# VectorE transposes squares of 32x32 for the norms' scales, the parameters and part of x

## The chip, the core and the metric

The kernel runs on one core of a Trainium2 chip. The core has a matrix engine (TensorE, "PE" in the profile; its weight loads are "PEld"), a vector engine (VectorE, "DVE"), an activation engine (ScalarE, "ACT"), GpSimd ("POOL") and a sync engine ("SP") that here only issues DMAs. Each engine runs its own instructions in the order in which the program wrote them; they wait for each other through semaphores. The metric is the time of one execution in microseconds on the device.

## What is computed

One layer of a decoder on 256 positions of 1024 columns, in float32: a norm, attention with 16 heads of 64, a projection and a residual, a second norm, a gated feed-forward net with a causal convolution of width 3, a residual and a last norm. With 256 positions there is one block of keys only, so the block-sparse attention is ordinary causal attention with a bias by distance.

```python
def rms_norm(x, g):
    y = xf * lax.rsqrt(jnp.mean(xf * xf, axis=-1, keepdims=True) + NORM_EPS)
    return (y * g.astype(jnp.float32)).astype(x.dtype)

y = rms_norm(h, attn_norm[i])
qkv = (y @ w_qkv[i]).reshape(B, S, 3, N_HEADS, HEAD_DIM)
o = moba_attention(q, k, v, rel_bias)      # softmax(q k / 8 + bias, causal) v
h = h + o.transpose(0, 2, 1, 3).reshape(B, S, D) @ w_o[i]
y = rms_norm(h, ffn_norm[i])
# conv_ffn: u = y @ w_up; u = conv over 3 positions + conv_b; (silu(gate) * val) @ w_down
h = h + conv_ffn(y, w_up[i], conv_w[i], conv_b[i], w_down[i])
return rms_norm(h, final_norm)
```

## The kernel before

**Layout.** x lies in `xs` as two row tiles of 128 positions by 1024 columns. A product needs its input with the contracted dimension on partitions, so the normed x is kept transposed in `yt`: 8 blocks of 128 columns, each 128 x 256 positions. The norm's per-column weight (`g1`, `g2`) is multiplied in when a block is transposed; its per-position scale (1 / root of the mean square) is not. It is multiplied in after the products: for V, whose positions lie on partitions, as a scalar per partition; for queries, keys and the feed-forward net, whose positions lie along the free dimension, it must stand in every partition as a row of 256 numbers (`rk`, `rq`, `rb2`).

**Split products.** TensorE multiplies in a shortened float format. Each operand is therefore split into a part in that format and the rest (`yt[:, 0]` and `yt[:, 1]`; `whi` and `wlo` for weights), and each product is three matmuls: first with first, rest with first, first with rest. ACT casts a weight tile to `whi` (line 144) and DVE subtracts to give `wlo` (line 157). One cast and one subtraction make a unit; `unit(n)` puts n of them where they are called, in the order of the table `groups`: V's weights, queries and keys by head pair, the output projection, then up and down. A raw weight tile is one of four; when its second unit is written, the next load is issued on SP's queue (`load_next`), and it starts when the tile's readers are done. SP's first loads are, in order: x's columns 0 to 255, weight rows for V, x's columns 256 to 511, weight rows for V, x's columns 512 to 1023 (line 187), the next weight rows for V (line 98), and so on.

**Order.** Nothing is scheduled by a planner: `manual_schedule` keeps the order of the code on every engine.
- V first: `transposed(k)` turns two blocks of x on TensorE into PSUM (line 260); ACT writes `yt[:, 0]` (264), DVE `yt[:, 1]` (267). Steps i = 0 to 3 of the loop at line 376 transpose the next two blocks, multiply the two blocks at hand with V's weights into four accumulators `acc`, and put units behind that.
- After the last step but one, ACT has the squares, DVE adds (`rstds`, 239), POOL raises to the power -0.5 (240), and DVE scales the identity with the result (`diagonals`, 252). `spread` multiplies ones with these on TensorE, which gives the scale in every partition; DVE copies it from PSUM to `rk` (404) and makes `rq` (405). V is read out of `acc` by ACT (401) and DVE (403).
- Heads follow in three steps of 2, 3 and 3 pairs: `project` gives a pair's queries and keys, which DVE multiplies with `rq` (439) and `rk` (442); `scores`, softmax, a turn of the weights (partly by a 32x32 transpose on DVE over all 128 partitions, line 484, and DMAs), and `mix` one step later, written out by ACT (525) and DVE (526).
- Parameters of the feed-forward net (convolution weights, its bias, `ffn_norm`) are loaded as rows and transposed by `other_params` on TensorE (225), in step i = 2 of V's loop; ACT copies them to `params` (226) and scales `g2` (227).
- The second norm: TensorE transposes blocks 4 to 7, and multiplies the first two tiles of `up` (`first[0]`, `first[1]`, two PSUM banks). Between their halves stands the second `spread`; DVE copies it to `rb2` (700). For each tile j, DVE reads the bank as `u` = bank x `rb2` (656), and the convolution and gate follow. There are two banks, so tile j + 2 waits for the `u` of tile j.
- The end: `finish` is called for each row tile. It takes POOL's power (739), scales the row (DVE 512 columns at line 743, ACT twice 256 at line 746) and issues three DMAs (747, 748).

Of the kernel before, what the change touches and what calls it, by code (L numbers as in the profile page):

```python
# [8 lines left out]
F32 = mybir.dt.float32  # L9
# [5 lines left out]
P = 128  # L15
S = 256
# [31 lines left out]
def tile_block(ctx: ExitStack, tc, x, attn_norm, w_qkv, w_o, rel_bias, ffn_norm, w_up, conv_w,  # L48
# [20 lines left out]
    def spare():  # L69
        return psT.tile([P, 512], F32, name="spare")  # L70

    def mm(o, lhsT, rhs, start, stop):
        nc.tensor.matmul(o, lhsT, rhs, start=start, stop=stop, skip_group_check=True)  # L73
# [148 lines left out]
    def other_params():  # L222
        ps = spare()[:, :2 * P].rearrange("p (a b) -> p a b", a=2)
        for i in range(2):
            nc.tensor.transpose(ps[:, i, :], rows[:, i, :], ident)  # L225
        nc.scalar.activation(params, ps, AF.Copy)
        nc.scalar.activation(g2, g2, AF.Copy, scale=math.sqrt(D))
# [5 lines left out]
    small.tile([P, 104], F32, name="gap", bufs=1)  # L233
# [9 lines left out]
    def spread(d, ps):  # L243

        for t in range(NT):
            mm(ps[:, t * P:(t + 1) * P], ones, d[t], True, True)
        return ps[:, :S]

    def diagonals(r):
        d = [small.tile([P, P], F32, name=f"diag{t}", bufs=1) for t in range(NT)]  # L250
        for t in range(NT):
            nc.vector.tensor_scalar(d[t], ident, r[:, t:t + 1], None, op0=ALU.mult)
        return d
# [15 lines left out]

    def transposed(k, g, ps=None):  # L270

        ps = flipped_rows(k, ps)
        for part in (columns_hi, columns_lo):
            for a in range(2):
                part(ps, k, g, a)
# [79 lines left out]

    ps = flipped_rows(0)
# [19 lines left out]
    for i in range(4):  # L376
        if i < 3:
            transposed(2 * i + 2, g1)
        if i == 2:
            other_params()  # L380
        for kk in range(2):
            k = 2 * i + kk
            if k:
                rows_product(accs, yt[:, :, k, :], ("v", i), kk, CHAINS, False, k == KD - 1)
        if i:
            unit(2)
        else:
            for _ in range(2):
                split_hi()
                split_lo()  # L390
        if i == 1:
            nc.scalar.activation(junk[0], xt[0], AF.Square, accum_out=stat[:, 0, 0:1])
        if i == 2:
            nc.scalar.activation(junk[1], xt[1], AF.Square, accum_out=stat[:, 0, 1:2])
            r1 = rstds()
            d1 = diagonals(r1)
    ps = spread(d1, bank())
# [6 lines left out]
    nc.vector.tensor_copy(rk, ps)  # L404
# [131 lines left out]
    for step in STEPS:  # L536
# [10 lines left out]
        for j, p in enumerate(step):  # L547
            split_to(("qk", p))
            for which in range(2):
                state["by"] = nc.gpsimd if last and 2 * j + which < 3 else nc.vector  # L550
                project(p, which)
                if not (step == STEPS[1] and (j, which) == (2, 1)):
                    unit(2 if not last and which == 0 else 1)
# [142 lines left out]
    up_k(1, first[1], range(0, 4))  # L696
    up_k(0, first[0], range(4, 8))
    ps = spread(diagonals(rstds()), acc())
    unit(2)
    nc.vector.tensor_copy(rb2, ps)  # L700
    up_k(1, first[1], range(4, 8))
# [32 lines left out]
    def finish(t, n):  # L734
# [8 lines left out]
        nc.vector.tensor_scalar(o[:, 512:], xg[t][:, 512:], r, None, op0=ALU.mult)  # L743
        for q, b in ((nc.sync, 0), (nc.scalar, 256)):
            c = slice(b, b + 256)
            nc.scalar.activation(o[:, c], xg[t][:, c], AF.Copy, scale=r)  # L746
            q.dma_start(rows[:, c], o[:, c])
        nc.sync.dma_start(rows[:, 512:], o[:, 512:])
# [66 lines left out]
```

## Time and profile before

| | before |
|---|---|
| time, median of 3 runs | 301.33 us (299.57 to 301.43) |
| the profiled execution's own time | 301.26 us |
| its span, from the first instruction to the last | 299.5 us |
| TensorE (PE) busy | 291.8 us, 97% |
| VectorE (DVE) busy | 229.9 us, 77% |
| ScalarE (ACT) busy | 170.7 us, 57% |
| mean granted TensorE clock | 0.996 of full |

All engines' times are microseconds from the span's start. A row of the trace gives the start, the length, the engine, the line, the operation, the tile written and the tiles read, the shape and the count. Brackets at its end hold the time for which the engine was idle before the row and what ended that. Neighbouring equal instructions are merged into one row with a count (x2), whose length goes from the first one's start to the last one's end. In the chain of waits a row holds the start, the length and the place of a piece of the work that ended last. A row of stretches gives each engine's busy time in a stretch, with the number of instructions, then the granted clock, the DMA engines' busy share and GB/s.

### The profile page before, as it was taken

The page shows a single profiled execution, that of the slowest core. Times are in us where ns is not written, and L with a number is a line of the kernel's source. Part 1 is how long each engine was busy: PE and PEld are TensorE (multiplying, and loading weights), DVE is VectorE, ACT ScalarE, POOL GpSimd, SP SyncE. Part 2 cuts the span into 40 slices and gives each one's busy share as a digit, 9 for nine tenths or more (in the row PEclk, how much of TensorE's full clock was granted, in tenths as well). Part 3 has the DMA queues.
Part 4 walks back from the last instruction along what each step waited for, and adds up shares of the span by engine and source line. Part 5 has one row for each costly group of instructions (what it writes and reads, how often), then busy time and mean ns, then how long its engine had stood idle before and what let it go on. Part 6 is the DMA issues. An engine that isn't in the chain of part 4 may idle for free.

```text
span 299.5 us, 5466 instructions
## 1 busy us (share of the span) xinstructions
PE 291.8 (97%) x2116; PEld 269.6 (90%) x2116; DVE 229.9 (77%) x428; ACT 170.7 (57%) x311; POOL 32.1 (11%) x61
## 2 busy tenths in 40 slices
PE   8999999999999999999999999999999999999992
PEld 7888989989978789998989899999989898999881
DVE  2666888569598585999895959988795959599751
ACT  4485837339265677477582727756474727275241
POOL 4703006418200001000000000000000000000010
PEclk9999999999999999999999999999999999999998
DMA  6999397798896964274939092976364748400011
GB/s 222 414 385 297 133 368 218 188 407 214 246 383 155 325 211 177 88 239 141 344 128 327 24 349 63 317 239 229 130 220 135 265 142 279 144 0 2 0 70 70
DMA packets 44245, 62.07 MB, mean 207 GB/s; under 512 B 1772, under 2 KB 37308, under 8 KB 44220
## 3 DMA queue, kind: packets, MB, share of 16 engines
q1 hardware_dynamic: 42492, 58.43, 58.1%
q0 software_dynamic: 848, 2.65, 2.9%
q10 hardware_dynamic: 880, 0.66, 0.9%
q8 instruction: 16, 0.26, 0.3%
q14 instruction: 9, 0.07, 0.1%
HBM read 57.90 MB, written 3.83 MB: 206 GB/s over the span
## 4 chain that ended last, share of the span: by engine, by line
PE 93%; issue 2%; DMA 1%; DVE 1%; ACT 1%; POOL 0%; POOLq 0%
PE acc L73 43%; PE bank L73 42%; PE spare L73 7%; DMA xs<-in_x_dram 1%; PE bank L260 1%; PE acc L260 1%; DVE xs L731 0%; POOL rf L739 0%; ACT o L746 0%; ACT junk L726 0%; DVE xg L723 0%; PE spare L512 0%; POOLq L811 0%; DVE kt L442 0%; PE spare L225 0%
## 5 line engine op out<-in xcount | busy, mean ns | idle before, releaser
L73 PE MATMUL bank<-yt,whi 128*128 128x256 f32 x704 | 120.6, 276 | 0.0
L157 DVE TENSOR_TENSOR wlo<-raw,whi 128x1024 fp32r<-128x1024 f32 x90 | 107.2, 1219 | 1.5 <-issue 0.9
L73 PEld LDWEIGHTS bank<-yt,whi 128*128 128x128 f32 x704 | 106.0, 188 | 0.0
L144 ACT ACTIVATE whi<-raw 128x1024 fp32r<-128x1024 f32 x96 | 95.3, 1047 | 9.5 <-DMA raw<-in_w_qkv_dram 4.9
L73 PE MATMUL bank<-yt,wlo 128*128 128x256 f32 x352 | 97.2, 276 | 0.0
L73 PEld LDWEIGHTS bank<-yt,wlo 128*128 128x128 f32 x352 | 66.1, 188 | 0.0
L660 ACT ACTIVATE cv<-u,params 128x256 f32<-128x256 f32 x44 | 24.1, 594 | 64.6 <-DVE u L656 64.6
L73 PE MATMUL acc<-whi,at 128*128 128x512 f32 x164 | 44.8, 390 | 0.0
L73 PEld LDWEIGHTS acc<-whi,at 128*128 128x128 f32 x164 | 30.1, 188 | 5.8
L656 DVE TENSOR_TENSOR u<-bank,rb 128x512 f32<-128x512 f32 x22 | 15.2, 691 | 21.1 <-PE bank L73 21.1
L73 PE MATMUL acc<-yt,whi 128*128 128x256 f32 x160 | 27.3, 276 | 0.0
L73 PE MATMUL acc<-wlo,at 128*128 128x512 f32 (+1 forms) x90 | 26.1, 370 | 0.0
L73 PEld LDWEIGHTS acc<-yt,whi 128*128 128x128 f32 x160 | 24.1, 188 | 0.0
L672 DVE SCALAR_TENSOR_TENSOR cv<-u,params,cv 128x254 f32<-128x254 f32 x44 | 21.3, 483 | 1.6
L73 PE MATMUL acc<-yt,wlo 128*128 128x256 f32 x80 | 22.1, 276 | 0.0
L670 DVE SCALAR_TENSOR_TENSOR cv<-u,params,cv 128x255 f32<-128x255 f32 x44 | 21.1, 478 | 0.3 <-ACT cv L660 0.3
L739 POOL TENSOR_TENSOR rf<-rf,minus_half 128x1 f32<-128x1 f32 x2 | 1.5, 740 | 174.7 <-DVE rf L738 174.7
L73 PE MATMUL acc<-whi,ot 128*128 128x512 f32 x64 | 20.2, 396 | 0.0
L73 PEld LDWEIGHTS acc<-wlo,at 128*128 128x128 f32 x90 | 16.9, 188 | 3.5
L73 PE MATMUL acc<-whi,yt 128*128 128x512 f32 x64 | 19.1, 427 | 0.0
L471 ACT ACTIVATE weights<-weights,nz 128x128 f32<-128x128 f32 (+1 forms) x32 | 14.1, 443 | 5.6 <-DVE nz L467 5.6
L73 PE MATMUL spare<-yt,whi 128*128 128x256 f32 x96 | 16.8, 280 | 0.0
(119 smaller groups left out, 334.9 us busy)
## 6 DMA issues: line engine op xcount, KB each, us to landing
raw<-in_w_up_dram SPq DMA_DIRECT2D x22, 1024.0 KB, 5.7
raw<-in_w_down_dram SPq DMA_DIRECT2D x11, 1024.0 KB, 6.2
raw<-in_w_qkv_dram SPq DMA_DIRECT2D x10, 1024.0 KB, 7.9
raw<-in_w_o_dram SPq DMA_DIRECT2D x4, 1024.0 KB, 5.3
weights<-turned SPq DMA_DIRECT2D x7, 384.0 KB, 3.5
turned<-weights SPq DMA_DIRECT2D x24, 96.0 KB, 1.9
raw<-in_w_qkv_dram SPq DMA_DIRECT2D x4, 512.0 KB, 8.3
bias<-line_d POOLq DMA_DIRECT2D x8, 256.0 KB, 4.6
```

The source lines that it names most:

```text
L73: nc.tensor.matmul(o, lhsT, rhs, start=start, stop=stop, skip_group_check=True)
L144: nc.scalar.activation(h, src, AF.Copy)
L157: state["by"].tensor_tensor(l, src, h, op=ALU.subtract)
L260: nc.tensor.transpose(ps[:, a, t * P:(t + 1) * P], xt[t][:, (k + a) * P:(k + a + 1) * P], ident)
L471: nc.scalar.activation(sc[p][:, a, c], sc[p][:, a, c], AF.Exp, bias=nm[:, j], accum_out=z[:, j])
L656: nc.vector.tensor_tensor(u, ps, rb2.unsqueeze(1).to_broadcast([P, 2, S]), op=ALU.mult)
L660: nc.scalar.activation(c[:, a, :], u[:, a, :], AF.Identity, scale=w2, bias=b)
L670: nc.vector.scalar_tensor_tensor(c[:, a, 1:], u[:, a, :S - 1], w1, c[:, a, 1:], op0=ALU.mult, op1=ALU.add)
L672: nc.vector.scalar_tensor_tensor(c[:, a, 2:], u[:, a, :S - 2], w0, c[:, a, 2:], op0=ALU.mult, op1=ALU.add)
L739: nc.gpsimd.tensor_tensor(r, r, minus_half, op=ALU.pow)
```

## The change

VectorE's transpose turns squares of 32 x 32. The change reads a square from one group of 32 partitions and writes it to another, sixteen times for a block of 128 x 128, and so makes a whole transpose without TensorE. It does that in four places.

- `spread(r, to)` reads the scale of 32 positions, repeated 32 times along the free dimension, and writes it to 32 partitions of the row: 16 instructions of 32 x 64 for two row tiles. It stands for the diagonals, the two products with ones and the copy out of PSUM, at both norms. At the second norm it now stands ahead of the two units.
- `blocks_of_x` transposes x's last 256 columns into a tile of the attention's pool, in two parts of 8 instructions of 32 x 128, ahead of the columns of steps i = 0 and 1. In step i = 2 ACT and DVE read that tile instead of PSUM.
- `other_params` transposes the parameters with 16 instructions of 32 x 64. It has moved from V's loop to the second step of heads, between the query and the key product of pair 3.
- `finish` sends a row tile out as two pieces of 256 columns that DVE scales (SP's queue) and one of 512 that ACT scales (ACT's queue).

Beside these, V's last product on TensorE is cut into two halves of 256 columns, and a filler tile (`gap`) grows by what the diagonals took.

```diff
--- before.py
+++ after.py
@@ -220,17 +220,18 @@
         nc.scalar.activation(g1, ps[:, :KD], AF.Copy, scale=math.sqrt(D))
 
     def other_params():
-        ps = spare()[:, :2 * P].rearrange("p (a b) -> p a b", a=2)
-        for i in range(2):
-            nc.tensor.transpose(ps[:, i, :], rows[:, i, :], ident)
-        nc.scalar.activation(params, ps, AF.Copy)
+
+        for a in range(4):
+            for b in range(4):
+                nc.vector.transpose(params[b * 32:(b + 1) * 32, :, a * 32:(a + 1) * 32],
+                                    rows[a * 32:(a + 1) * 32, :, b * 32:(b + 1) * 32])
         nc.scalar.activation(g2, g2, AF.Copy, scale=math.sqrt(D))
 
 
 
     act.tile([P, 48], F32, name="skew")
     yt = act.tile([P, 2, KD, S], F32R, name="yt")
-    small.tile([P, 104], F32, name="gap", bufs=1)
+    small.tile([P, 360], F32, name="gap", bufs=1)
     stat = small.tile([P, 2, NT], F32, name="stat", bufs=1)
 
     def rstds():
@@ -240,17 +241,13 @@
         nc.gpsimd.tensor_tensor(r, r, minus_half.to_broadcast([P, NT]), op=ALU.pow)
         return r
 
-    def spread(d, ps):
-
-        for t in range(NT):
-            mm(ps[:, t * P:(t + 1) * P], ones, d[t], True, True)
-        return ps[:, :S]
-
-    def diagonals(r):
-        d = [small.tile([P, P], F32, name=f"diag{t}", bufs=1) for t in range(NT)]
-        for t in range(NT):
-            nc.vector.tensor_scalar(d[t], ident, r[:, t:t + 1], None, op0=ALU.mult)
-        return d
+    def spread(r, to):
+
+        to = to.rearrange("p (t q) -> p t q", t=NT)
+        for a in range(4):
+            block = r[a * 32:(a + 1) * 32, :].unsqueeze(2).to_broadcast([32, NT, 32])
+            for b in range(4):
+                nc.vector.transpose(to[b * 32:(b + 1) * 32, :, a * 32:(a + 1) * 32], block)
 
     def flipped_rows(k, ps=None):
 
@@ -267,12 +264,14 @@
         nc.vector.scalar_tensor_tensor(yt[:, 1, k + a, :], ps[:, a, :], g[:, k + a:k + a + 1],
                                        yt[:, 0, k + a, :].bitcast(F32), op0=ALU.mult, op1=ALU.subtract)
 
-    def transposed(k, g, ps=None):
-
-        ps = flipped_rows(k, ps)
+    def columns(flipped, k, g):
         for part in (columns_hi, columns_lo):
             for a in range(2):
-                part(ps, k, g, a)
+                part(flipped, k, g, a)
+
+    def transposed(k, g, ps=None):
+
+        columns(flipped_rows(k, ps), k, g)
 
     junk = [act.tile([P, D], BF16, name=f"junk{t}") for t in range(NT)]
 
@@ -352,6 +351,17 @@
     def first_products(half, w, n):
         for t in range(NT):
             mm(accs[t, half], yt[:, n, 0, t * P:(t + 1) * P], w[g, 0][:, HALVES[half]], w is hi and n == 0, False)
+
+    last_x = ap.tile([P, 768], F32, name="weights", bufs=6)[:, :512].rearrange("p (a b) -> p a b", a=2)
+
+    def blocks_of_x(k, part):
+
+        to = last_x.rearrange("p a (t c) -> p a t c", t=NT)
+        rows_of = xs[:, :, k * P:(k + 2) * P].rearrange("p t (a c) -> p a t c", a=2)
+        for b in range(4):
+            for a in (2 * part, 2 * part + 1):
+                nc.vector.transpose(to[b * 32:(b + 1) * 32, :, :, a * 32:(a + 1) * 32],
+                                    rows_of[a * 32:(a + 1) * 32, :, :, b * 32:(b + 1) * 32])
 
     ps = flipped_rows(0)
     keep_warm(MORE_WARM)
@@ -374,14 +384,15 @@
         first_products(half, lo, 0)
     load_next()
     for i in range(4):
-        if i < 3:
+        if i < 2:
+            blocks_of_x(KD - 2, i)
             transposed(2 * i + 2, g1)
         if i == 2:
-            other_params()
+            columns(last_x, KD - 2, g1)
         for kk in range(2):
             k = 2 * i + kk
             if k:
-                rows_product(accs, yt[:, :, k, :], ("v", i), kk, CHAINS, False, k == KD - 1)
+                rows_product(accs, yt[:, :, k, :], ("v", i), kk, CHAINS, False, k == KD - 1, k == KD - 1)
         if i:
             unit(2)
         else:
@@ -393,15 +404,13 @@
         if i == 2:
             nc.scalar.activation(junk[1], xt[1], AF.Square, accum_out=stat[:, 0, 1:2])
             r1 = rstds()
-            d1 = diagonals(r1)
-    ps = spread(d1, bank())
+    spread(r1, rk)
     for t, half in CHAINS:
         c = slice(half * 512, (half + 1) * 512)
         if half == 0:
             nc.scalar.activation(vs[:, t, c], accs[t, half], AF.Copy, scale=r1[:, t:t + 1])
         else:
             nc.vector.tensor_scalar(vs[:, t, c], accs[t, half], r1[:, t:t + 1], None, op0=ALU.mult)
-    nc.vector.tensor_copy(rk, ps)
     nc.vector.tensor_scalar(rq, rk, HD ** -0.5, None, op0=ALU.mult)
     unit(2)
 
@@ -549,6 +558,8 @@
             for which in range(2):
                 state["by"] = nc.gpsimd if last and 2 * j + which < 3 else nc.vector
                 project(p, which)
+                if step == STEPS[1] and (j, which) == (1, 0):
+                    other_params()
                 if not (step == STEPS[1] and (j, which) == (2, 1)):
                     unit(2 if not last and which == 0 else 1)
         for p in last:
@@ -693,12 +704,12 @@
     for k in (4, 6):
         transposed(k, g2, ps=acc())
     squares(1, 1)
-    up_k(1, first[1], range(0, 4))
-    up_k(0, first[0], range(4, 8))
-    ps = spread(diagonals(rstds()), acc())
+    spread(rstds(), rb2)
+    for ks in (range(0, 4), range(4, 8)):
+        if ks[0]:
+            up_k(0, first[0], ks)
+        up_k(1, first[1], ks)
     unit(2)
-    nc.vector.tensor_copy(rb2, ps)
-    up_k(1, first[1], range(4, 8))
     for j in range(NF):
         if j < 2:
             gates(j, first[j])
@@ -740,12 +751,11 @@
         weighted(t, LAST[t], last[t])
         o = fp.tile([P, D], F32, name="o", bufs=2)
         rows = out[0, t * P:(t + 1) * P, :]
-        nc.vector.tensor_scalar(o[:, 512:], xg[t][:, 512:], r, None, op0=ALU.mult)
-        for q, b in ((nc.sync, 0), (nc.scalar, 256)):
-            c = slice(b, b + 256)
-            nc.scalar.activation(o[:, c], xg[t][:, c], AF.Copy, scale=r)
-            q.dma_start(rows[:, c], o[:, c])
-        nc.sync.dma_start(rows[:, 512:], o[:, 512:])
+        for c in QUARTERS:
+            nc.vector.tensor_scalar(o[:, c], xg[t][:, c], r, None, op0=ALU.mult)
+            nc.sync.dma_start(rows[:, c], o[:, c])
+        nc.scalar.activation(o[:, :512], xg[t][:, :512], AF.Copy, scale=r)
+        nc.scalar.dma_start(rows[:, :512], o[:, :512])
```

On VectorE, the rows before, from the weight rests of V's second group to the scale `rq` at the first norm (`yt` are the columns, `wlo` the weight rests, `vs` is V):

```order
L157 TENSOR_TENSOR wlo<-raw,whi 128x1024 x2
L267 SCALAR_TENSOR_TENSOR yt<-bank,g_119,yt 128x256 x2
L157 TENSOR_TENSOR wlo<-raw,whi 128x1024 x2
L267 SCALAR_TENSOR_TENSOR yt<-bank,g_119,yt 128x256 x2
L157 TENSOR_TENSOR wlo<-raw,whi 128x1024 x2
L239 SCALAR_TENSOR_TENSOR rstd<-stat 128x2
L252 TENSOR_SCALAR diag_351<-ident,rstd 128x128
L252 TENSOR_SCALAR diag_352<-ident,rstd 128x128
L157 TENSOR_TENSOR wlo<-raw,whi 128x1024 x2
L403 TENSOR_SCALAR vs<-acc,rstd 128x512 x2
L404 COPY rk<-bank 128x256
L405 TENSOR_SCALAR rq<-rk 128x256
```

and the same stretch now, beginning one pair of columns earlier (`weights` is the tile that takes the transposed x, line 264 the columns, 240 the sum of squares, 413 V):

```order
L363 STREAM_TRANSPOSE weights<-xs 32x4x32 x8
L264 SCALAR_TENSOR_TENSOR yt<-bank,g_119,yt 128x256 x2
L157 TENSOR_TENSOR wlo<-raw,whi 128x1024 x2
L363 STREAM_TRANSPOSE weights<-xs 32x4x32 x8
L264 SCALAR_TENSOR_TENSOR yt<-bank,g_119,yt 128x256 x2
L157 TENSOR_TENSOR wlo<-raw,whi 128x1024 x2
L264 SCALAR_TENSOR_TENSOR yt<-weights,g_119,yt 128x256 x2
L157 TENSOR_TENSOR wlo<-raw,whi 128x1024 x2
L240 SCALAR_TENSOR_TENSOR rstd<-stat 128x2
L157 TENSOR_TENSOR wlo<-raw,whi 128x1024 x2
L250 STREAM_TRANSPOSE rk<-rstd 32x2x32 x16
L413 TENSOR_SCALAR vs<-acc,rstd 128x512 x2
```

Two groups of 8 transposes stand ahead of columns that V's products need, and 16 stand ahead of V's read-out where two diagonals and a copy stood.

On VectorE at the second norm, from the sum of squares to the first tile's convolution, the rows before (`rb` is the row of scales, `u` the tile read out of its bank):

```order
L239 SCALAR_TENSOR_TENSOR rstd<-stat 128x2
L252 TENSOR_SCALAR diag_1510<-ident,rstd 128x128
L252 TENSOR_SCALAR diag_1511<-ident,rstd 128x128
L157 TENSOR_TENSOR wlo<-raw,whi 128x1024 x2
L700 COPY rb_1413<-acc 128x256
L656 TENSOR_TENSOR u<-bank,rb_1413 128x512
L157 TENSOR_TENSOR wlo<-raw,whi 128x1024
```

and now:

```order
L240 SCALAR_TENSOR_TENSOR rstd<-stat 128x2
L250 STREAM_TRANSPOSE rb_1446<-rstd 32x2x32 x16
L157 TENSOR_TENSOR wlo<-raw,whi 128x1024 x2
L667 TENSOR_TENSOR u<-bank,rb_1446 128x512
L157 TENSOR_TENSOR wlo<-raw,whi 128x1024
```

Sixteen transposes take the place of two diagonals ahead of the weight rests; the copy behind them is gone.

## The prediction

> **What bounds the kernel now.** I read the page's busy shares first, then the chain of waits.
>
> ```profile
> PE 291.8 (97%) x2116; PEld 269.6 (90%) x2116; DVE 229.9 (77%) x428; ACT 170.7 (57%) x311; POOL 32.1 (11%) x61
> PE 93%; issue 2%; DMA 1%; DVE 1%; ACT 1%; POOL 0%; POOLq 0%
> ```
>
> TensorE (PE) is busy 97% of the span and is 93% of the chain that ends last. So an instruction that PE loses is worth its own length, if whatever takes over its work is ready when PE reaches the place. What PE loses stands in the chain in order of time (start, length):
>
> ```profile
> 20.19 0.44 PE bank L260 x4
> 20.63 0.22 PE spare L225 x2
> ...
> 31.85 0.44 PE bank L73 x4
> ...
> 121.26 0.44 PE acc L73 x4
> ```
>
> These are the transposes of x's last 256 columns, of the parameters, and the spreading of the first and the second norm's scales. They sum to 0.44 + 0.22 + 0.44 = 1.10 us before the scores and 0.44 us at the second norm, 1.54 us in all, 0.5% of the time. 1% is about 3.0 us, and that is about what a measurement of this kernel can tell from no change.
>
> **The price of one small transpose.** VectorE (DVE) gets 64 of them: 16 with 128 elements per partition (x, two groups of 8), and three groups of 16 with 64 elements. The trace has none of 32 partitions, only seven of 128 x 768.
>
> ```profile
> 49.87 0.98 DVE L484 STREAM_TRANSPOSE weights<-weights 128x768 f32<-128x768 f32 x1
> 50.77 0.15 DVE L479 RECIPROCAL bank<-nz 128x4 f32<-128x4 f32 x1
> ```
> ```profile
> L157 DVE TENSOR_TENSOR wlo<-raw,whi 128x1024 fp32r<-128x1024 f32 x90 | 107.2, 1219 | 1.5 <-issue 0.9 <-ACT whi L144 0.5
> L350 DVE TENSOR_TENSOR wlo<-raw,whi 128x512 fp32r<-128x512 f32 x4 | 2.7, 683 | 0.0
> ```
> ```profile
> 0.83 0.17 DVE L199 MEMSET ones<- 128x128 f32 x1 [0.83 <-PEq L802]
> 1.10 0.27 DVE L200 MEMSET rows<- 64x256 f32 x1
> 1.44 0.06 DVE L313 MEMSET stat<- 128x2 f32 x1
> ```
>
> 512 more elements cost 1219 - 683 = 536 ns, 1.05 ns each; the transpose's 980 ns less 768 of these leaves 0.18 us fixed. That makes 0.24 us for 64 elements and 0.31 us for 128 (estimates from these rows). What counts is the step to the next one. Between instructions that start at partition 0, the next begins 0.08 us before the end (49.87 + 0.98 against 50.77): steps of 0.16 and 0.23 us, the lower bound. The only rows whose start partition changes (0, then 64, then 0) begin 0.10 and 0.07 us behind the end: 0.32 and 0.39 us, the upper bound. Each square of this change writes at another start partition than at least one neighbour. I take the next to begin as the last ends, between the two: 0.25 and 0.32 us.
>
> [...]
>
> **Up to the scores (10 to 43 us).** DVE's rows, with its idle time in brackets:
>
> ```profile
> 12.40 0.88 DVE L267 SCALAR_TENSOR_TENSOR yt<-bank,g,yt 128x256 fp32r<-128x256 f32 x2 [2.58 <-ACT yt L264]
> 13.35 2.36 DVE L157 TENSOR_TENSOR wlo<-raw,whi 128x1024 fp32r<-128x1024 f32 x2
> ...
> 21.54 0.88 DVE L267 SCALAR_TENSOR_TENSOR yt<-bank,g,yt 128x256 fp32r<-128x256 f32 x2 [2.62 <-ACT yt L264]
> ...
> 24.99 0.16 DVE L239 SCALAR_TENSOR_TENSOR rstd<-stat 128x2 f32<-128x2 f32 x1 [0.30 <-ACT junk L394]
> 26.00 0.74 DVE L252 TENSOR_SCALAR diag<-ident,rstd 128x128 f32<-128x128 f32 x2 [0.85 <-POOL rstd L240]
> 26.40 2.35 DVE L157 TENSOR_TENSOR wlo<-raw,whi 128x1024 fp32r<-128x1024 f32 x2
> 30.52 0.75 DVE L403 TENSOR_SCALAR vs<-acc,rstd 128x512 f32<-128x512 f32 x1 [1.77 <-PE acc L73]
> 31.89 0.75 DVE L403 TENSOR_SCALAR vs<-acc,rstd 128x512 f32<-128x512 f32 x1 [0.62 <-PE acc L73]
> 32.56 0.41 DVE L404 COPY rk<-bank 128x256 f32<-128x256 f32 x1
> ...
> 40.51 0.42 DVE L439 TENSOR_TENSOR qt<-acc,rq 128x256 f32<-128x256 f32 x1 [0.87 <-PE acc L73]
> ...
> 43.23 0.42 DVE L442 TENSOR_TENSOR kt<-acc,rk 128x256 f32<-128x256 f32 x1
> ```
>
> The last row is the one for which PE's scores wait; what DVE does late up to there, PE does late. Behind the new transposes are queued, in this order: the columns and weight rests of V's steps, and at the norm V's evictions, the scale rq, more rests and the first query and key products. The first eight transposes need the last piece of x, which the trace gives no landing for. It is bounded by its neighbour:
>
> ```profile
> 3.88 0.53 SPq L98 DMA_DIRECT2D raw<-in_w_qkv_dram  x1
> ```
> ```profile
> raw<-in_w_qkv_dram SPq DMA_DIRECT2D x1, 512.0 KB, 8.3
> ```
> ```profile
> 10.00:12.00 2.00, 2.00 (x12) 1.69 (x11) 0.00 (x0) 0.47 (x2) 2.00 (x18) 1.00 1.03 423
> ```
>
> These are the issue of the piece right behind it on SP's queue (weight rows for V), its landing, and DMA and engine work from 10 to 12 us, with GB/s last. The piece lands 8.3 us after 3.88, at 12.2; its 512 KB at 423 GB/s take 1.2 us, so x is there at about 10.9 (estimate). Eight by 0.32 end at 13.5. The columns due at 12.40 are 1.1 us late, and the first weight rest behind them ends at 13.35 + 1.22 + 1.06 = 15.63, where PE wants it here:
>
> ```profile
> 15.46 0.62 PE L73 MATMUL acc<-wlo,yt 128*128 128x512 f32 x2
> ```
>
> So 0.2 us of waiting on PE (none at a step of 0.23). From there I balance DVE's time. Added: 16 x 0.32 + 16 x 0.25 = 9.12. Removed: the two diagonals (26.00 to 26.40, 0.40) and the copy to rk with its gap, 0.45, together 0.85. To be filled: of 2.58 only 10.9 to 12.40, 1.50, then 2.62 + 0.30 + 0.85 + 1.77 + 0.62 + 0.87 = 7.03, together 8.53. 9.12 - 0.85 - 8.53 = -0.26: DVE's row at 43.23 comes 0.26 us earlier, where PE alone could be 1.10 - 0.2 = 0.9 earlier. **Term: -0.26 us**; bounds -1.10 (step 0.16) and +1.98 (0.32). The last product of V in two halves has the same columns and costs nothing; at worst 0.1.
>
> **Parameters (54 to 63 us).** 16 x 0.25 = 4.0 us go between the query and the key product of head pair 3:
>
> ```profile
> 56.42 0.42 DVE L442 TENSOR_TENSOR kt<-acc,rk 128x256 f32<-128x256 f32 x1 [2.29 <-PE acc L73]
> ...
> 59.14 0.42 DVE L439 TENSOR_TENSOR qt<-acc,rq 128x256 f32<-128x256 f32 x1 [1.16 <-PE acc L73]
> ...
> 61.86 0.42 DVE L442 TENSOR_TENSOR kt<-acc,rk 128x256 f32<-128x256 f32 x1 [1.16 <-PE acc L73]
> ```
> ```profile
> 62.67 0.38 ACT L525 ACTIVATE ot<-spare 128x256 fp32r<-128x256 f32 x1 [7.60 <-PE spare L73]
> 63.20 1.58 PE L73 MATMUL acc<-kt,qt 64*128 64x128 f32 x16
> ```
>
> They leave 4.0 - 2.29 = 1.7 us, which the two waits of 1.16 take in before 63.20. On ACT the scaling of g2 now waits for them, with three weight casts behind it, in an idle stretch of 7.60 us. Term 0. Were that cover gone, it would be the 1.7.
>
> **Second norm.** The squares stand directly behind POOL's power, where the diagonals began, and ahead of two weight rests:
>
> ```profile
> 118.85 0.48 DVE L252 TENSOR_SCALAR diag<-ident,rstd 128x128 f32<-128x128 f32 x2 [0.85 <-POOL rstd L240]
> 119.25 2.35 DVE L157 TENSOR_TENSOR wlo<-raw,whi 128x1024 fp32r<-128x1024 f32 x2
> ...
> 122.20 0.69 DVE L656 TENSOR_TENSOR u<-bank,rb 128x512 f32<-128x512 f32 x1
> ```
> ```profile
> 124.27 0.39 PE L73 MATMUL bank<-yt,whi 128*128 128x256 f32 x2
> ```
>
> 118.85 + 16 x 0.25 = 122.85; the rests take 2.27 to the next start; u runs from 125.12 to 125.81. The row at 124.27 is PE's third projection, which writes the bank that this u empties: now it has 1.4 us to spare, then it could start at 124.27 - 0.44 = 123.83 and stands until 125.85, a wait of 2.0. **Term: 125.85 - 124.27 = +1.58 us**; bounds +0.14 (0.16) and +2.70 (0.32). The squares wait for POOL as the diagonals did, so that wait is not new; behind them stand the rests and u, and behind u the scaling on ACT. DVE is then 125.12 - 122.20 = 2.9 us behind its rows and PE 1.6; that the next u, due a whole projection later, is still in time I take from that distance. If not, PE waits at most the difference, 1.3 us, once more.
>
> **The end.**
>
> ```profile
> 290.09 0.63 ACT L726 ACTIVATE junk<-xs 128x512 bf16<-128x512 f32 x1 [1.22 <-DVE xs L731]
> ...
> 295.01 0.91 ACT L746 ACTIVATE o<-xg,rf 128x256 f32<-128x256 f32 x2 [0.86 <-POOL rf L739]
> ```
> ```profile
> 295.98 0.37 SPq L748 DMA_DIRECT2D out_dram<-o  x1
> ```
>
> The 256 KB leave last now, at 295.98. Then ACT's one pass of 512 (0.63, row of that shape) releases 256 KB at about 295.7, and SP's second quarter follows its first at about 295.8 with half the bytes. **Term: -0.3 us** (-0.4 to 0; no landing from ACT's queue is in the rows).
>
> **Sum.** -0.26 + 0 + 1.58 - 0.3 = +1.0 us. The profiled execution took 301.26 (span 299.5), the median of the runs is 301.33, so the base is the same: 302.3 us. For a step s (and s + 0.07 for x) the same sum is 48 s - 11.0 once DVE is the bound, zero at 0.23; the likeliest case's own range, 0.23 to 0.28, is 301.3 to 303.7.
>
> **Rivals.** *Overlapped steps* (0.16, 0.23): the balance has 3.1 us over, PE keeps all of 1.10, the second norm adds 0.14, the end takes 0.3: -1.26, 300.0 us. For it: all transposes on record overlap; against it: the memset rows. *Late steps*: each square begins behind the other's end as the memsets do (0.32, 0.39): +1.98 + 2.70 - 0.3 = +4.4, 305.6 us, slower. It decides from a step of 0.29, where 48 s - 11.0 passes 3.0. Against it: two rows at the kernel's start, where issue may be slow. *Nothing in the way*: squares so cheap (under 0.12) that the second norm hides them too: -1.54 - 0.3, 299.4 us. Against it: 0.18 us fixed.
>
> **Chances.** Forecast 0.50, overlapped 0.25, late 0.20, nothing in the way 0.05. The range runs from 299.5, under the overlapped case, to 305.0, into the late one, leaving out most of that and half of the last case. Faster by over 1% (under 298.3) is beyond every case: 0.03; slower by over 1% (over 304.3) is the late case: 0.20; within 1%: 0.77.
>
> **What would show it.** Steps of the new transposes read off DVE's rows decide between the cases. PE's waits should show DVE's u at the second norm with about 2.0 us (0.6 if overlapped, 3.1 if late), a wait for the weight rest near 15.5, and none from 54 to 63. The forecast is wrong if x lands elsewhere than near 10.9, or if DVE still idles by microseconds between 13 and 43 while PE waits.

## The result and the profile after

The changed kernel took 305.12 us (median of 6 runs, 302.17 to 305.77), the kernel before 300.74 us (6 runs, 299.57 to 301.49). The ratio is 1.0132, 95% interval 1.0083 to 1.018: the change makes the kernel slower by 0.8 to 1.8%. The profiled execution took 305.77 us, its span is 304.0 us. Of the experiments' runs below, two slow ones (303.54 us of the kernel before, 308.47 us of the one with the weight units first) are left out of the ratios, not of the medians.

The page of the changed kernel, busy shares and chain of waits by engine:

```profile
PE 292.0 (96%) x2103; PEld 268.8 (88%) x2103; DVE 243.6 (80%) x488; ACT 170.1 (56%) x308; POOL 34.1 (11%) x61
PE 64%; DVE 15%; DMA 9%; issue 5%; SPq 2%; ACT 2%; POOL 1%; POOLq 0%; DVEq 0%; ACTq 0%
```

PE has 13 matmuls fewer and is as busy as before (292.0 against 291.8 us). DVE has gained 13.7 us, and the chain now runs through DVE for 15% where it was 1%. The groups of the new transposes, with the mean length of one behind the busy time, and then four rows of DVE in order of time:

```profile
L363 DVE STREAM_TRANSPOSE weights<-xs 32x128 f32<-32x128 f32 x16 | 4.8, 303 | 1.3 <-DMA xs<-in_x_dram 1.1
L250 DVE STREAM_TRANSPOSE rb<-rstd 32x64 f32<-32x64 f32 x16 | 3.8, 236 | 1.1 <-POOL rstd L241 0.8
```
```profile
10.66 2.51 DVE L363 STREAM_TRANSPOSE weights<-xs 32x128 f32<-32x128 f32 x8 [1.10 <-DMA xs<-in_x_dram]
...
119.59 3.98 DVE L250 STREAM_TRANSPOSE rb<-rstd 32x64 f32<-32x64 f32 x16 [0.85 <-POOL rstd L241]
123.60 2.36 DVE L157 TENSOR_TENSOR wlo<-raw,whi 128x1024 fp32r<-128x1024 f32 x2
125.88 0.68 DVE L667 TENSOR_TENSOR u<-bank,rb 128x512 f32<-128x512 f32 x1
```

Sixteen squares take 3.98 us, eight of x 2.51 us: steps of 0.25 and 0.31 us. In the trace each begins 13 to 14 ns behind the end of the one ahead (up to 32 ns among the parameters' squares). So none overlaps the next, and none leaves a gap of 0.07 us either; the groups at the first norm (3.99 us) and of the parameters (3.98 us) are alike in length. This is the forecast's case.

What PE waits for, in total, in times, and the longest, and PE's rows at these places:

```profile
PE bank L73 <- DVE u L667: 1.9, 1, 1.9
...
PE acc L73 <- DVE kt L451: 0.8, 1, 0.8
PE acc L73 <- DVE wlo L157: 0.8, 1, 0.8
...
PE acc L73 <- DVE yt L264: 0.5, 1, 0.5
PE bank L73 <- DMA weights<-turned: 0.5, 1, 0.5
```
```profile
13.74 0.73 PE L73 MATMUL acc<-whi,yt 128*128 128x512 f32 x2 [0.48 <-DVE yt L264]
15.26 0.74 PE L73 MATMUL acc<-wlo,yt 128*128 128x512 f32 x2 [0.79 <-DVE wlo L157]
```
```profile
126.62 0.50 PE L73 MATMUL bank<-yt,whi 128*128 128x256 f32 x2 [1.90 <-DVE u L667]
...
127.41 0.39 PE L73 MATMUL bank<-yt,whi 128*128 128x256 f32 x2
...
128.34 0.63 PE L73 MATMUL bank<-yt,whi 128*128 128x256 f32 x2
```

The wait for `u` is the one forecast (2.0). By starts of PE's work, the third projection begins 126.62 - 112.77 = 13.85 us after the first `up`, against 124.27 - 112.02 = 12.25 before: 1.60 us more, where the forecast's term was 1.58. But about 1.1 us behind it a pair of the same matmuls takes 0.63 us instead of 0.39. Stretches of 1 us, granted clock in the third column from the end:

```profile
127.00:128.00 1.00, 1.00 (x11) 1.00 (x10) 1.00 (x2) 1.00 (x3) 0.00 (x0) 0.90 0.00 0
128.00:129.00 1.00, 1.00 (x7) 1.00 (x7) 0.96 (x3) 1.00 (x2) 0.00 (x0) 0.50 0.20 27
129.00:130.00 1.00, 1.00 (x6) 1.00 (x6) 0.96 (x3) 0.90 (x2) 0.00 (x0) 0.50 0.74 216
130.00:131.00 1.00, 1.00 (x7) 1.00 (x6) 1.00 (x2) 0.00 (x0) 0.00 (x0) 0.50 1.08 384
131.00:132.00 1.00, 1.00 (x10) 1.00 (x10) 1.00 (x3) 0.71 (x2) 0.00 (x0) 0.90 1.18 399
```

The clock is at half for 3.41 us (127.79 to 131.21 in the trace). PE counts as busy all the while, so the busy shares do not show this loss: half of 3.41, 1.7 us (an estimate).

The profile of the kernel before hides something too, at its start. PE's first eight products there, and then in the kernel before with only the second norm's squares (an experiment below), whose code is the same up to that norm:

```profile
6.28 3.75 PE L73 MATMUL acc<-whi,yt 128*128 128x512 f32 x8
```
```profile
6.13 2.08 PE L73 MATMUL acc<-whi,yt 128*128 128x512 f32 x8 [0.16 <-DVE whi L354]
```

In the one profiled execution of the kernel before, PE ran these at about half speed (0.44 us from one to the next, 0.24 in the changed kernel), up to 10.1 us. Of the ten profiles of this study, two began so; the other eight ran them in 2.1 to 2.7 us. That moved everything in the prediction's base up to the scores. Starts of PE's work at four places, and the span:

| us | before, as profiled | before with the second norm's squares | after |
|---|---|---|---|
| first query product | 32.05 | 30.15 | 31.20 |
| first scores | 43.71 | 41.81 | 43.05 |
| first product of `up` | 112.02 | 110.74 | 112.77 |
| first product of `down` | 135.15 | 137.20 | 139.52 |
| span | 299.49 | 301.55 | 304.00 |

Against the profile of before, the changed kernel gains 0.66 us up to the scores. Against an execution of the same code that began at full speed, it loses 43.05 - 41.81 = 1.24 us. At the second norm (from `up` to `down`) it takes 26.75 instead of 23.13 us, 3.62 more. The later medians of the kernel before, 299.79 us (24 runs) and 299.99 us (19 runs), lie nearer to a start at full speed: 301.26 less the 1.90 us by which the scores start earlier in the second column is 299.36. (At `up` that column is only 1.28 us ahead, since its products from 43 to 62 us run 4% slower; the last section has this.)

### The profile page after: what moved, and what is told of

It is laid out like the page before. It is cut to its first block, busy times and chain, and to the rows that moved or that the text cites. A ratio compares the mean times of both kernels' runs of the same rounds, so it can differ in the third digit from the quotient of the medians.

```text
span 304.0 us, 5492 instructions
## 1 busy us (share of the span) xinstructions
PE 292.0 (96%) x2103; PEld 268.8 (88%) x2103; DVE 243.6 (80%) x488; ACT 170.1 (56%) x308; POOL 34.1 (11%) x61
## 4 chain that ended last, share of the span: by engine, by line
PE 64%; DVE 15%; DMA 9%; issue 5%; SPq 2%; ACT 2%; POOL 1%; POOLq 0%; DVEq 0%; ACTq 0%
PE bank L73 38%; PE acc L73 24%; DVE wlo L157 3%; DMA raw<-in_w_qkv_dram 3%; DMA xs<-in_x_dram 2%; DMA raw<-in_w_o_dram 2%; DVE weights L491 1%; DVE weights L493 1%; DVE rk L250 1%; DVE yt L264 1%; DVE rb L250 1%; POOL rstd L241 1%; DVE weights L363 1%; DVE params L226 1%; DMA weights<-turned 1%
## 5 line engine op out<-in xcount | busy, mean ns | idle before, releaser
L73 PE MATMUL bank<-yt,whi 128*128 128x256 f32 x704 | 122.5, 279 | 1.9 <-DVE u L667 1.9
L73 PEld LDWEIGHTS bank<-yt,whi 128*128 128x128 f32 x704 | 107.4, 190 | 2.1 <-DVE u L667 2.1
L73 PEld LDWEIGHTS bank<-yt,wlo 128*128 128x128 f32 x352 | 66.8, 190 | 0.0
L73 PE MATMUL acc<-whi,yt 128*128 128x512 f32 x64 | 17.7, 398 | 1.0 <-DVE whi L345 0.6
```

## The experiments

Each ratio is to the kernel before, run beside it on the same chip: the first four kernels against a median of 299.79 us, the last four against 299.99 us. The ratios and their intervals are those on record; they are not the quotients of these medians, which differ from them by up to 0.0021. Each run also lists its mean granted clock; one fall to half for 3.41 us takes 0.006 off it.

### The second norm given back to TensorE

```diff
-    spread(rstds(), rb2)
-    for ks in (range(0, 4), range(4, 8)):
-        ...
+    up_k(1, first[1], range(0, 4))
+    up_k(0, first[0], range(4, 8))
+    ps = spread_pe(diagonals(rstds()), acc())
     unit(2)
+    nc.vector.tensor_copy(rb2, ps)
+    up_k(1, first[1], range(4, 8))
```

> The changed kernel, but the second norm's scale is spread by diagonals and products with ones as before. Theory (clock): in the changed kernel's trace PE stands 1.9 us at the second norm for DVE's u, and the granted clock then is 0.50 from 127.7 to 131.1; the wait costs 1.6 us net and the half clock about 2.0 us more. Without the wait both go: 304.0 - 1.6 - 2.0 = about 300.4 us of span, no 0.50 between 120 and 135, time within 0.5 us of before. Rival (late DVE): the 2.0 us behind the wait come from DVE, which is 2.9 us behind there; they go too, so this run alone does not separate the two, but it gives the second norm's whole share.

Measured: 301.70 us (10 runs), ratio 1.0045 (1.0013 to 1.0076). From `up` to `down` it takes 23.13 us again, to the hundredth the kernel before. So 3.4 of the 4.4 us lie at the second norm, by the medians, 2.6 by the ratios. What is left, 1.0013 to 1.0076, lies in the other parts; this profile began at half speed as that of before did, and PE does not wait for x's columns or the weight rest in it. Its scores begin at 42.91 us, 0.80 before the 43.71 of the kernel before: in such a start x, the first norm and the parameters by squares do gain time up to the scores.

### The second norm's squares alone

The kernel before with `spread` by squares at the second norm, in the order of the changed kernel.

```diff
-    up_k(1, first[1], range(0, 4))
-    up_k(0, first[0], range(4, 8))
-    ps = spread(diagonals(rstds()), acc())
+    spread_sq(rstds(), rb2)
+    for ks in (range(0, 4), range(4, 8)):
+        ...
     unit(2)
-    nc.vector.tensor_copy(rb2, ps)
-    up_k(1, first[1], range(4, 8))
```

> The kernel before, with the second norm's scale spread by 16 squares on DVE ahead of the two units, and nothing else of the change. My forecast for this part alone was +1.58 us. Theory (clock): +1.6 for the wait and +2.0 for half clock behind it, about 303.1 us of span (299.5 + 3.6), ratio about 1.012. If the clock is not involved: +1.6, about 301.1 us.

Measured: 302.13 us (10 runs), ratio 1.0086 (1.0052 to 1.012). What PE waits for, longest first, and its row behind the squares:

```profile
PE bank L73 <- DVE u L664: 1.9, 1, 1.9
```
```profile
124.59 0.50 PE L73 MATMUL bank<-yt,whi 128*128 128x256 f32 x2 [1.90 <-DVE u L664]
```

The same wait, and the same fall: half the clock for 3.41 us from 125.21. From `up` to `down` it takes 26.46 us, 3.33 more than before. Yet the median rose by 2.3 us. The listed clocks say why: three of the ten runs have a mean clock of 0.990 or 0.991 (302.91, 303.33 and 305.24 us), the other seven 0.995 to 0.997 (median 301.90). Of the changed kernel's six runs three are at 0.989 to 0.991 (305.13, 305.43, 305.77). So the clock seems to fall behind the wait in some of the executions only; the runs that were not profiled show no wait, and their clocks alone say so. The fall is not all that differs between executions either: one of the seven took 304.24 us at 0.997. Seven runs at 301.90 less 299.79 give 2.1 us for the wait without the fall, against 1.60 us by the starts of PE's work (124.59 - 110.74 = 13.85 us up to the third projection, 12.25 before). Behind the third projection's start this profile loses 1.73 us, half of 3.41.

### PE kept busy in that wait

```diff
+    filler = acc()
+    for _ in range(8):
+        mm(filler[:, :P], ones, ones, True, True)
     unit(2)
```

The eight products of ones (sixteen matmuls in the trace) are not used by anything.

> The changed kernel with 8 filler products (ones by ones, 128x128, read by nobody) behind the second projection, where PE stands for u. PE has more work and DVE the same. Theory (clock): PE no longer stands for 1.9 us, the granted clock stays 1.00 and some 2.0 us go: about 302 us of span. Rival (late DVE): the wait for u is the same length and everything behind it comes as late as before, so 304.0 or a little more.

The row of the products that fill the wait:

```profile
124.91 1.95 PE L73 MATMUL acc<-ones 128*128 128x128 f32 x16
```

Measured: from `up` to `down` 24.86 us instead of 26.75, with a granted clock of 1.00 from 124 to 130 us. Eight useless products made this stage 1.89 us faster. The third projection begins as long after the first `up` as in the changed kernel (126.97 - 113.11 = 13.86 us), so all of it is won behind the wait. 1.7 us are the clock at half; the remaining 0.2 can come from products that run 4% slower from 131 to 140 us in the changed kernel's profile, 0.3 us, and not in this one (last section). The time, though, was 303.96 us (4 runs), ratio 1.0118 (1.0077 to 1.0159). In its profile the clock fell at another place, behind the two waits for x:

```profile
14.42 0.74 PE L73 MATMUL acc<-whi,yt 128*128 128x512 f32 x2 [1.09 <-DVE yt L264]
15.94 0.74 PE L73 MATMUL acc<-wlo,yt 128*128 128x512 f32 x2 [0.78 <-DVE wlo L157]
16.52 1.66 PE L73 MATMUL acc<-whi,yt 128*128 128x512 f32 x4
```
```profile
17.00:18.00 1.00, 1.00 (x4) 0.71 (x4) 0.93 (x5) 0.33 (x2) 0.00 (x0) 0.50 1.09 384
```

The query products began at 33.23, 2.0 us later than in the changed kernel. That explains the profiled run alone: two of the other three list a mean clock of 0.996 and 0.997, too high for such a fall, and took 303.36 and 304.29 us. What they lose, and where, stays open. So the filler shows what the fall costs at the second norm, and the time does not show that it helps the kernel.

### The weight units ahead of the second norm's squares

```diff
-    spread(rstds(), rb2)
+    r2 = rstds()
+    unit(2)
+    spread(r2, rb2)
     for ks in (range(0, 4), range(4, 8)):
         ...
-    unit(2)
```

> The changed kernel with the two units ahead of the second norm's squares instead of behind them, so that DVE fills POOL's 0.85 us with a weight rest. u comes about 0.8 us earlier, PE stands about 1.1 us instead of 1.9. Theory (clock): if a stand of 1.1 us is too short to lower the clock, the span falls by 0.8 + 2.0 to about 301.2 us; if not, by 0.8 to 303.2. Rival (late DVE): it falls by 0.8 or a little more, with the clock at 1.00 or 0.50 alike.

Measured: 302.81 us (9 runs), ratio 1.0086 (1.0057 to 1.0115). PE waits 1.0 us for `u`, the clock holds in the profile, and `up` to `down` takes 23.99 us, 0.86 more than before:

```profile
124.79 0.51 PE L73 MATMUL bank<-yt,whi 128*128 128x256 f32 x2 [1.03 <-DVE u L667]
```

The weight rests stand in what was POOL's time (0.85 us of idle DVE), and that is all they can win: squares and rests are 6.3 us in a row, however they are ordered.

### x's squares alone

The kernel before with `blocks_of_x` and V's last product in two halves; norms and parameters stay on TensorE.

```diff
-        if i < 3:
+        if i < 2:
+            blocks_of_x(KD - 2, i)
             transposed(2 * i + 2, g1)
         if i == 2:
+            columns(last_x, KD - 2, g1)
             other_params()
         ...
-                rows_product(accs, yt[:, :, k, :], ("v", i), kk, CHAINS, False, k == KD - 1)
+                rows_product(accs, yt[:, :, k, :], ("v", i), kk, CHAINS, False, k == KD - 1, k == KD - 1)
```

> The kernel before, with one part of the change alone: x's last 256 columns by the two groups of eight squares, and V's last product in two halves; both norms and the parameters stay on TensorE. Theory A (the squares stand ahead of the columns and the weight rest that TensorE waits for, and the execution profiled of the kernel before hid that because its TensorE began at half speed): TensorE waits 0.4 to 0.5 us for the columns near 13.7 and 0.7 to 0.8 us for the weight rest near 15.3, the query and key products begin at 30.7 to 31.2 us (30.15 in the profiled execution of the kernel before with only the second norm's squares, whose first part is that of the kernel before), and the time is 0.5 to 1.5 us above the kernel before's; about 2 us more where the granted clock falls behind these waits. Theory B (the prediction's working): TensorE waits 0.2 us near 15.5 and has 0.44 us of transposes less, so the time is the kernel before's less 0.2 us, 0.1% under it.

Measured: 300.94 us (6 runs), ratio 1.0024 (1.0002 to 1.0045). PE's rows:

```profile
12.40 0.72 PE L73 MATMUL acc<-whi,yt 128*128 128x512 f32 x2
13.68 0.74 PE L73 MATMUL acc<-whi,yt 128*128 128x512 f32 x2 [0.56 <-DVE yt L267]
15.20 0.74 PE L73 MATMUL acc<-wlo,yt 128*128 128x512 f32 x2 [0.78 <-DVE wlo L157]
```

Theory A holds: the query products begin at 31.51 us, 1.36 later than 30.15. Two products 0.23 us apart should end in a step of 0.46, and the two steps are 1.28 and 1.52: PE loses 0.82 + 1.06 = 1.88 us, against which stand the four transposes that it saves. DVE has time to spare afterwards (3.6 us of waits from 25 to 41 us), and PE does not get it back: what PE has lost by 15 us stays lost.

### x's squares behind the products and splits of V's first two steps

```diff
         if i < 2:
-            blocks_of_x(KD - 2, i)
             transposed(2 * i + 2, g1)
         ...
         if i:
             unit(2)
         ...
+        if i < 2:
+            blocks_of_x(KD - 2, i)
```

> The changed kernel with each of the two groups of eight squares of x moved behind the products and weight splits of V's first and second step, where it stood ahead of them. Theory A (order of VectorE's queue is what costs): the waits of TensorE near 13.7 (0.5) and 15.3 (0.8) go, the query and key products begin at 30.2 to 30.7 us (31.2 in the changed kernel), and the time is 0.6 to 1.0 us under the changed kernel's, 304.1 to 304.5 by its 305.1; the wait of 1.9 us at the second norm and the clock's fall behind it stay. Theory B (VectorE's work in all is what costs up to the scores): the squares only move the waiting, the scores begin no earlier than in the changed kernel (43.0) and the time stays at 305.1.

Measured: 307.11 us (4 runs), ratio 1.0227 (1.021 to 1.0243), 2.0 us above the changed kernel. The early waits are gone, as theory A has it, and the query products begin at 29.76 us. But the scores begin at 43.60, later than 43.05, as theory B has it. What PE waits for, and two stretches:

```profile
PE acc L73 <- DVE kt L452: 2.6, 1, 2.6
PE bank L73 <- DVE u L668: 1.9, 1, 1.9
```
```profile
45.00:46.00 1.00, 1.00 (x6) 0.52 (x3) 0.00 (x0) 0.34 (x1) 0.00 (x0) 0.50 1.06 322
46.00:47.00 1.00, 1.00 (x7) 1.00 (x6) 0.25 (x1) 1.00 (x2) 0.00 (x0) 0.50 1.06 367
```

The wait has only moved, from two of half a microsecond to one of 2.6 us ahead of the scores, and behind that one the clock falls as well (44.68 to 48.09). All four runs have a mean clock of 0.986 to 0.990. So with both x and the first norm as squares, DVE's whole work up to the scores is the bound, in both of the orders that were run.

### The same with the second norm given back

Both edits shown above, in one kernel.

> The changed kernel with the second norm's scale spread by TensorE as before, and x's squares behind the products and splits of V's first two steps. Theory A: no wait over 0.3 us is left on TensorE up to the scores and none at the second norm, so that the time is the kernel before's within 0.5 us, and 0.7 to 1.0 us under the changed kernel with only the second norm given back (301.7). Theory B (VectorE's work in all is the bound up to the scores): no gain over that kernel, 301.5 to 302.

Measured: 302.75 us (4 runs), ratio 1.0099 (1.0078 to 1.012), no better than with the second norm alone given back (1.0045). Theory A falls, and this other place does not rescue x's squares; no third place was tried. The wait:

```profile
PE acc L73 <- DVE kt L464: 2.4, 1, 2.4
```
```profile
44.00:45.00 1.00, 1.00 (x8) 0.91 (x10) 0.00 (x0) 0.44 (x1) 0.00 (x0) 0.50 1.11 340
```

### The first norm and the parameters alone

The kernel before with `spread` by squares at the first norm, and with the parameters' squares at their new place; x, the second norm and the end as before.

```diff
-            d1 = diagonals(r1)
-    ps = spread(d1, bank())
+    spread_sq(r1, rk)
 ...
-    nc.vector.tensor_copy(rk, ps)
```

> The kernel before, with the first norm's scales and the parameters by squares (the two parts that the prediction put behind other work), x, the second norm and the end as before. Theory A (these two are hidden): TensorE loses 0.44 + 0.22 us of work, the scores begin 0.3 to 0.66 us earlier against an execution that begins alike, and the time is 0.3 to 0.66 us under the kernel before's (0.1 to 0.2%). Theory B (VectorE is the bound between 25 and 43 us: 4.0 us of squares for 0.85 us of diagonals and copy): TensorE waits for the query and key products' banks, the scores begin as late or later and the time is 0 to 0.5 us above.

Measured: 299.82 us (12 runs), ratio 0.9998 (0.9983 to 1.0013). The scores begin at 41.31 us, 0.50 before 41.81, so the squares are hidden there as theory A says; PE's row:

```profile
41.31 0.93 PE L73 MATMUL acc<-kt,qt 64*128 64x128 f32 x8 [0.52 <-DVE kt L447]
```

The wait of 0.52 is in the second norm's experiment too, where DVE writes no squares up to there. Later this profile loses more than that: from the scores to `up` it takes 69.53 us, against 68.31 before. PE waits 0.4 us for turned weights near 82 us, and its products run 4% slower for 18 us (last section). The interval reaches from a gain of 0.5 us to a loss of 0.4, and so neither theory is settled by the time.

No kernel here beats the one before by more than the measurement tells. The single costs (1.0086, 1.0024 and 0.9998) multiply to 1.0108, inside the interval of the whole change. The new order of the last stores was in no experiment by itself.

## Why the prediction was right or wrong

The forecast was 302.3 us, 1.0 above the base, in a range up to 305.0; it was 305.12. "Slower by over 1%" had a chance of 0.20 and came, by the median ratio; its interval begins at 0.8%. The number is near that of the rival with late steps (305.6), but that mechanism was not it: the steps were the forecast's. What failed is the term up to the scores (1.5 us), the end (0.4 us), and two things at which the sum put nothing: the clock's fall behind the wait at the second norm (1.7 us in part of the executions) and a wait for turned weights (0.5 us).

- **The step of the squares**: forecast 0.25 and 0.32 us, measured 0.25 and 0.31. The "overlapped" and the "late" rival and "nothing in the way" fall.
- **x's landing**: forecast about 10.9 us, the first square begins at 10.66.
- **Up to the scores** (term -0.26 us): wrong, by about 1.5 us. The step that failed is the local one, "0.2 us of waiting on PE": it takes 12.40 and 15.46 from an execution in which PE had lost time before. In a start at full speed DVE writes the columns here (the kernel before with the second norm's squares):

```profile
10.48 0.88 DVE L275 SCALAR_TENSOR_TENSOR yt<-bank,g,yt 128x256 fp32r<-128x256 f32 x2 [0.93 <-ACT yt L272]
```

  That is ahead of x's landing at 10.66, so the columns stand behind that and eight squares, at 13.20 in the changed kernel, and nothing of the 1.50 us taken as filled ("of 2.58 only 10.9 to 12.40") is there. The balance without it, 9.12 - 0.85 - 7.03 with the other idle times as they were (0.16 + 0.48 + 2.07 + 0.31 + 0.85 + 1.67 + 0.62 + 0.87 = 7.03 in that execution), gives +1.24 us, and the scores came 1.24 us late. That it fits to the hundredth is luck: in the changed kernel DVE still idled 0.62 us for POOL's power, which the balance takes as filled. But the method comes near, and what was wrong is its base, the less usual execution. The one profile of an experiment that began slowly too, with the second norm given back, bears this out: its scores begin 0.80 us earlier than in the kernel before, and no wait near 15.5 us is in it. The term's upper bound, +1.98, held the value, but as a case of late steps.
- **Parameters** (term 0): right for the stretch that it is about. The first `mix` begins 18.05 us after the scores with the second norm given back, as in the kernel before; in the changed kernel it is 18.67 us, as with the second norm's squares alone, where no parameter was moved, and both have the slower products there. What I did not name is the wait of 0.5 us for turned weights near 84 us. A wait of 0.2 to 0.5 us stands there in five of the seven kernels with the parameters moved and in none without; its cause wasn't isolated.
- **Second norm** (term +1.58 us, wait 2.0): the wait was 1.90, and the third projection came 1.60 us later. The mechanism and its size were right, and the next `u` was in time, as assumed. The sum left out what follows a wait, a term put at nothing without a reason: PE's clock at half for 3.41 us, 1.7 us. By the listed clocks it fell in 3 of the 6 runs of the changed kernel; these took 305.44 us in the mean, the other three 303.77.
- **The end** (term -0.3 us): wrong; nothing was gained. From the start of PE's last matmul to the span's end 6.24 us passed, before 6.13. The last piece on SP's queue did leave earlier, 2.19 us behind the end of PE's last matmul (at 300.23 us) instead of 2.34 (at 295.98), but the span then went on for 3.77 us instead of 3.51. The trace has no landing of this piece. The rows below give one landing each, that of the first row tile's last piece: half the bytes landed no sooner. Issues with KB and time to landing, of the changed kernel and of the one before:

```profile
out_dram<-o SPq DMA_DIRECT2D x4, 128.0 KB, 2.5
```
```profile
out_dram<-o SPq DMA_DIRECT2D x2, 256.0 KB, 2.5
```

- **The sum, made again** for the changed kernel's profile, on a start at full speed (299.36): +1.24 up to the scores; +1.41 from there to `up`, of which 0.62 are the slower products of 45 to 62 us and 0.5 the wait for turned weights; +3.62 to `down` (1.60 up to the third projection, 1.7 for the clock at half, 0.3 for slower products); +0.14 to the end. Together that is +6.41 and 305.77, the profiled 305.77. The median is lower: the clock does not fall in every execution.

## What to carry to other kernels

An instruction taken off the busiest engine is a gain only if the engine that takes it over has idle time ahead of the moment at which the first one wants the result (at the second norm, where VectorE idled for 0.85 us, 0.44 us less work on TensorE came with a wait of 1.90); idle time behind that moment, or the mean over the stage, hides nothing. One profiled execution is a poor base for a slack of a microsecond: before a term rests on when an engine reaches a place, look at how fast TensorE ran its first products, and at where the same place lies in another run. And price a stand of TensorE near 2 us at up to twice its length: here 1.9 us were followed by 3.41 us at half the clock, about 1.7 us more, by the listed clocks in 3 runs of 6.

## What the runs showed of the hardware

**The clock falls behind short waits.** Waits of 1.9 (three times), 2.6 and 2.4 us, and two of 1.09 and 0.78 us within 3.4 us, were each followed by half the granted clock for 3.41 us, beginning between 0.3 us ahead of the wait's end and 1.4 us behind it. A wait of 1.03 us (the weight units first), and two of 0.56 and 0.78 us (x's squares alone), were not, in the profiles. The traces also show when. In the changed kernel's the changes of the granted clock come at 4.91, 127.79, 131.21 and 301.87 us, which is 36, 1 and 50 times 3.413 us apart; in that of the kernel before they come at 10.13 and 296.85 us, 84 times. In the 3.41 us ahead of each of the six falls that begin before PE's last matmul, PE stood idle for 1.8 to 2.3 us (1.90 in the changed kernel, 1.09 and 0.78 less a few hundredths with the filler); sums of waits up to 1.34 us, 0.56 and 0.78, had no fall behind them. By the listed clocks the fall came behind the wait of 1.9 us in 3 runs of 10 (the second norm's squares alone); what decides it is not shown, since the runs that were not profiled have no trace.

**The clock at the start differs from execution to execution.** In two of ten profiles the first eight products took 3.75 us, in eight 2.1 to 2.7 us. The column of the granted clock does not tell them apart: in the kernel before it shows 1.00 from 4 to 10 us too, since its record there begins at 10.13 us, with a value of 1.00; in the changed kernel it begins at 4.91. In the other late one, with the second norm given back, the four products behind the eight, from 9.98 us, took 1.33 us, against 1.08 or 1.09 in the eight. PE had no idle time in the 3.41 us up to 10.13 in the kernel before, nor in those up to 4.91 in the changed kernel. The two late profiles have waits of 0.28 us (for x, up to 4.45) and of 0.36 us (for `whi`, up to 6.43). Whether such small waits in the first 7 us decide it stays open: the changed kernel waited 0.57 us for `whi`, up to 6.14, and its eight products took 2.08 us. No run tested it by itself.

**A step of 117.8 ns.** In four kernels' profiles a stretch of products of 128x256 runs with a step of about 117.8 ns instead of 113.3, at a granted clock of 1.00: from 45 to 62 us and from 131 to 140 in the changed kernel, from 62 to 80 in that of the first norm and the parameters, from 43 to 62 in that of the second norm's squares, and from 30 us on in that with x later and the second norm given back. It costs 4%, 0.7 us in a stretch of 17 us. What causes it stays open.
